# Low halves of 68 projection weights: kept in DRAM by the context's mixer, loaded again by the latents' mixer

## The chip, the core and the metric

The kernel runs on one core of a Trainium2 chip. TensorE (PE) multiplies matrices, VectorE (DVE) and ScalarE (ACT) do elementwise work, GpSimd (POOL) issues the indirect gathers and a few other transfers, and SyncE (SP) issues most loads. The metric is the device time of one execution in microseconds (us); smaller is better.

## The reference, cut to what matters

Two layers run over 512 latent tokens and 256 context tokens of width 1024. Each layer has a mixer and then a product-key expert layer ("PEER").

```
p  = h  @ w_in[l]                      # latents, 512 tokens
pc = hc @ w_in[l]                      # context, 256 tokens, the same weights (layer 0)
ml_c, state = mlstm(pc, zero_state)    # the context's scan state goes into the latents' scan
ml_x, _     = mlstm(p, state)
y = sum over 4 branches z_i of sigmoid(gate_i(p)) * (z_i @ w_branch[i]);  out = y @ w_out
x = x + mod * out
...
e, g = product-key top-16 of 128 x 128 keys, for each of 8 heads      # 128 rows per token
a = gelu(u_tab[e] . h) * g;  x = x + mod * (a @ v_tab[e])             # PEER
```

In layer 0 the context goes through the whole mixer too, with the weights that the latents use. In layer 1 the context needs only the scan state.

## The kernel before

Every weight of a mixer product is multiplied in two parts: `hi` is the fp32 weight cast to fp32r, `lo` is what the cast lost, also in fp32r. The activations are split in the same way (tiles `hh` and `hl`), and `mm3` issues three passes for each 128 rows of contraction: hi by hi, hi by lo, lo by hi.

`wload` brings one weight tile of 128 x 1024 fp32 (512 KB): a load on SP's queue into `wr`, `S.copy` (ACT) into `wh`, and `V.tensor_tensor` (DVE) into `wl`, with L299 and L300 in `split`. In both mixers of layer 0 the rings `wr`, `wh` and `wl` have three buffers each (`W_MIX`).

A tile scheduler fixes the order of the instructions on each engine when the program is built; at run time every engine works through its list in order and waits where it must. The program of layer 0 runs so:

1. The context's mixer (`mlstm`, then `ctx_merge`), with 256 columns per matmul: 68 calls of `wload`. In the middle of it `x_first` loads the latents on POOL's queue: `x`, and eight tiles `tB<-in_scT` (L233), two at a time, which DVE adds to `x`.
2. The context's `routing` (top-k). `s_bg` runs `mlstm_steps`, the first projections of the latents' mixer, beside it.
3. The latents' mixer, with 512 columns per matmul: the mLSTM scan (L452, L453) and its eight head steps, the four projections of `conv`, then four calls of `merge_one`. A call has eight gate projections, each evicted by ACT's sigmoid (`sg`), and two branch weights; `gmlp` and `fnet` come between the calls. `w_out` is last. This is again 68 calls of `wload`, on the same 68 tiles.
4. `peer_lat`, and then layer 1.

Beside 2 and 3 run the context's expert rows (`gather_ctx`), paced by `rows_bg`. Each `DMA_INDIRECT` of POOL brings 128 rows, 512 KB, into `ug` (a ring of 3) or `gat` (a ring of 9). DVE reduces each u tile against `hn` (L1034, 1.2 us), and PE accumulates the v tiles (L1068). These instructions stand at fixed places among the mixer's.

```
def tick(self, us):
    self.credit += us * self.rate
    while self.q and self.credit >= self.q[0][1]:
        self.credit -= self.q[0][1]
        self.step()
```

Of the kernel before, what the change touches and what calls it, by code (L numbers as in the profile page):

```python
# [11 lines left out]
F32 = mybir.dt.float32  # L12
# [49 lines left out]
def build(nc, tc, I, out):  # L62
    V, S, G, PE = nc.vector, nc.scalar, nc.gpsimd, nc.tensor
# [4 lines left out]
    pw = [None, 0, 0]  # L68
    pb = pool(name="pb", bufs=1)
    pd = pool(name="pd", bufs=2, space=bass.MemoryType.DRAM)  # L70
# [63 lines left out]
    class Background:  # L134
# [20 lines left out]
# [5 lines that stand above are left out]
            if not self.q:  # L160
                self.credit = 0.0
# [27 lines left out]
    def mk(p, shape, dt=F32, tag=None, bufs=None):  # L189
        nid[0] += 1  # L190
        kw = {} if bufs is None else {"bufs": bufs}
        return p.tile(list(shape), dt, name=f"{tag}_{nid[0]}", tag=tag, **kw)
# [74 lines left out]
    def held(d):  # L267

        if hold[0] is not None:
            tc.add_manual_dep(d.ins, hold[0].ins.name, SYNC, reason="leave the memory to the loads before")  # L270
# [27 lines left out]
    def split(hi, lo, src):  # L298
        S.copy(hi, src)  # L299
        V.tensor_tensor(lo, src, hi, ALU.subtract)  # L300

    def wload(src, kt, n):

        raw = mk(pw[0], [128, kt, n], F32, "wr", pw[1])
        held(nc.sync.dma_start(raw, src.rearrange("p (k n) -> p k n", n=n)))
        hi = mk(pw[0], [128, kt, n], F32R, "wh", pw[2])
        lo = mk(pw[0], [128, kt, n], F32R, "wl", pw[2])
        split(hi, lo, raw)
        tick(5.1 * T_of[0] / 512)
        return hi, lo  # L310

# [459 lines left out]
    def branch(i, l, C, h, T, tag="z"):  # L771
        ztag[0] = tag
        return BRANCH[i](l, C, h, T)

    def merge_one(l, i, first, y, z, h, T, gates=None):

        for half in range(2):
            wb = wload(I["w_branchT"][l, i, half], 2, 512)
            for q in range(4):
                dt = 4 * half + q  # L780
                if not gates:
                    sg = mk(pt, [128, T], F32, "sg")
                elif q % 2:
                    sg = sg2[:, 1]
                else:
                    sg2 = mk(gates[0], [128, 2, T], F32, gates[1 + dt // 2])
                    sg = sg2[:, 0]
                S.activation(sg, proj_T(l, h, OFF_G + i * D + 128 * dt, T), AF.Sigmoid)
                ps = psum()
                mm3(ps[:, :T], cols(wb, 128 * q, 128), z)  # L790
                if first:
                    V.tensor_tensor(y[:, dt, :], ps[:, :T], sg, ALU.mult)
                else:
                    V.tensor_tensor(sg, ps[:, :T], sg, ALU.mult)
                    V.tensor_tensor(y[:, dt, :], y[:, dt, :], sg, ALU.add)

    def y_parts(y, T):
        yh = mk(hpool[0], [128, KT, T], F32R, "hh")
        yl = mk(hpool[0], [128, KT, T], F32R, "hl")
        for k in range(KT):  # L800
            split(yh[:, k, :], yl[:, k, :], y[:, k, :])
        return [(yh[:, k, :], yl[:, k, :]) for k in range(KT)]

    def w_out(l, yp, mod, s, T, x_old, x):

        for dt in range(KT):
            w = wload(I["w_outT"][l, dt], KT, 128)
            ps = psum()
            mm3(ps[:, :T], cols(w, 0, 128), yp)
            V.scalar_tensor_tensor(x[:, dt, :], ps[:, :T], mod[:, 16 + dt, s:s + 1], x_old(dt),  # L810
                                   op0=ALU.mult, op1=ALU.add)
# [505 lines left out]
    @phase  # L1317
    def ctx_merge(l, C, mod, xc, hc, zc_fn, between, mod_ready):
        y = mk(ph[0], [128, KT, CTX], F32, "y")
        zpool[0] = ph[0]  # L1320
        end = conv(l, C, hc, CTX, ph[0])
        zs = {i: branch(i, l, C, hc, CTX, "z%d" % i) for i in (3, 1)}
        merge_one(l, 3, True, y, zs[3], hc, CTX)
        between()
        merge_one(l, 1, False, y, zs[1], hc, CTX)
        merge_one(l, 2, False, y, end(), hc, CTX)
        merge_one(l, 0, False, y, zc_fn(), hc, CTX)
        yp = y_parts(y, CTX)
        mod_ready()
        w_out(l, yp, mod, 1, CTX, lambda dt: xc[:, dt, :], xc)  # L1330
# [5 lines left out]
    with psum_pool(mm=3, sm=3, acc=2):  # L1336
# [3 lines left out]
        with spool("cxa", 1) as cxa:  # L1340
# [6 lines left out]
            use_bufs(cx, cx, CTX)  # L1347
            hc = norm_mod(xc, CTX, mod, 1, C["norm1_g"], 0)
            ada_bg.rate = ADA_RATE
            side[0] = "right"  # L1350
            zc, state = mlstm(0, C, hc, CTX, None, True, True, "zm")
            hold[0] = None
# [7 lines left out]

            hl = []
            ctx_merge(0, C, mod, xc, hc, lambda: zc, lat_norm, lambda: ada_bg.finish(ag[2]))
            cx_cm.__exit__(None, None, None)
            cx_cm, cx = open_pool("cx", "left")
            use_bufs(cx, cx, CTX)
# [216 lines left out]
```

## Time and profile before

| | us |
|---|---|
| median of 3 runs | 4453.28 (4445.75 to 4458.83) |
| the profiled execution | 4470.13 |
| its span, first to last instruction | 4468.4 |
| PE busy in it | 4184.9 (94%) |
| DVE busy in it | 3314.7 (74%) |
| DMA's mean rate over the span | 266 GB/s |

Busy time says how long an engine had work in it, not that it set the pace. A matmul of PE counts as busy until its modelled end. What a stretch is bound by is read from its own rows: the busy time of each engine in that stretch, the share of the 16 DMA engines that were busy, and the waits.

### The profile page before, as it was taken

The numbers are of one execution on the slowest core, as the hardware profiler recorded it, in microseconds if no ns is written. First come the engines' busy times: TensorE is split into PE (matmuls) and PEld (weight loads), VectorE is DVE, ScalarE is ACT, GpSimd is POOL, SyncE is SP. The second block draws the span as 40 slices with busy tenths as digits, with TensorE's granted clock in tenths as the row PEclk, the third lists the DMA queues.
The fourth block names the chain that finished last, engine by engine and source line by source line (L and its number), as shares of the span: only waits on it lengthen the run. The fifth ranks groups of instructions, "written<-read, shape, count | busy, mean of one in ns | idle before, by whom it ended". The sixth has DMA issues, their size and how long they took to land.

```text
span 4468.4 us, 61238 instructions
## 1 busy us (share of the span) xinstructions
PE 4184.9 (94%) x22364; PEld 3462.8 (77%) x22364; DVE 3314.7 (74%) x6764; ACT 1631.7 (37%) x2317; POOL 1314.7 (29%) x1061
## 2 busy tenths in 40 slices
PE   7889778988999999999999999999999999999998
PEld 4786555666678898788888766777799997888887
DVE  4764888866689596777777794464899996777775
ACT  3441222323334445333333332443335553333333
POOL 0000256652243430333333365000022222233231
PEclk9999868999999999999999999889999999999999
DMA  8546778986678996999989799213267889898894
GB/s 281 198 142 207 273 254 332 364 305 221 203 269 300 343 343 245 346 332 324 320 310 321 285 326 327 85 42 110 73 249 289 281 293 329 306 314 305 312 312 159
DMA packets 417342, 1187.41 MB, mean 266 GB/s; under 512 B 39441, under 2 KB 142609, under 8 KB 413969
## 3 DMA queue, kind: packets, MB, share of 16 engines
q1 hardware_dynamic: 263360, 633.62, 41.4%
q0 software_dynamic: 150928, 549.52, 34.1%
q8 instruction: 176, 2.88, 0.3%
q14 instruction: 126, 1.02, 0.1%
q10 hardware_dynamic: 2752, 0.37, 0.1%
HBM read 1092.40 MB, written 90.96 MB: 265 GB/s over the span
## 4 chain that ended last, share of the span: by engine, by line
PE 48%; issue 17%; DVE 12%; DMA 10%; POOL 6%; ACT 1%; POOLq 0%; DVEq 0%; another core or an unknown queue 0%; ACTq 0%; SPq 0%
PE mm L319 18%; PE s L319 12%; PE acc L1208 8%; POOL gat L924 4%; DMA gsr<-sp 3%; PE sm L1127 3%; PE acc L1068 2%; DMA vr<-in_peer_v 2%; DVE wl L300 2%; DMA gat<-in_peer_v,eu 1%; POOL ug L924 1%; PE mm L826 1%; DMA ug<-in_peer_u,hu 1%; DVE gat L955 1%; PE sm L835 1%
## 5 line engine op out<-in xcount | busy, mean ns | idle before, releaser
L299 ACT CAST wh<-wr 128x1024 fp32r<-128x1024 f32 x498 | 521.4, 1048 | 1140.5 <-PE mm L319 631.4
L300 DVE TENSOR_TENSOR wl<-wr,wh 128x1024 fp32r<-128x1024 f32 x498 | 607.2, 1220 | 322.4 <-ACT wh L299 298.3
L319 PE MATMUL s<-hh,wh 128*128 128x384 f32 x2048 | 702.1, 343 | 6.3 <-ACT gs L1151 6.3
L924 POOL DMA_INDIRECT gat<-in_peer_u,eu x256 | 329.2, 1286 | 1278.8 <-DVE pu L868 488.1
L319 PE MATMUL s<-hh,wl 128*128 128x384 f32 x2048 | 694.7, 339 | 3.6 <-DVE wl L300 3.6
L319 PE MATMUL s<-hl,wh 128*128 128x384 f32 x2048 | 693.1, 338 | 0.0
L1208 PE MATMUL acc<-vh,al 128*128 128x512 f32 x1536 | 604.6, 394 | 19.9 <-DVE al L300 19.8
L319 PE MATMUL mm<-hh,wl 128*128 128x512 f32 (+1 forms) x1552 | 582.9, 376 | 40.3 <-DVE wl L300 40.2
L319 PE MATMUL mm<-hh,wh 128*128 128x512 f32 (+1 forms) x1552 | 589.0, 381 | 24.2 <-ACT wh L299 8.3
L1208 PE MATMUL acc<-vl,ah 128*128 128x512 f32 x1536 | 603.2, 393 | 7.2 <-DVE vl L300 7.2
L1208 PE MATMUL acc<-vh,ah 128*128 128x512 f32 x1536 | 601.3, 393 | 9.1 <-ACT vh L299 7.9
L319 PE MATMUL mm<-hl,wh 128*128 128x512 f32 (+1 forms) x1552 | 582.7, 376 | 3.4 <-DVE hl L300 2.3
L924 POOL DMA_INDIRECT gat<-in_peer_v,eu x256 | 330.2, 1290 | 654.6 <-PE acc L1208 553.8
L299 ACT CAST vh<-vr 128x1024 fp32r<-128x1024 f32 x256 | 268.8, 1050 | 551.3 <-DMA vr<-in_peer_v 528.7
L924 POOL DMA_INDIRECT gat<-in_peer_v,ev x256 | 295.8, 1155 | 405.0 <-PE acc L1068 242.6
L319 PEld LDWEIGHTS s<-hh,wh 128*128 128x128 f32 x2048 | 386.3, 189 | 30.5 <-issue 10.9
L319 PEld LDWEIGHTS mm<-hh,wh 128*128 128x128 f32 x1552 | 304.6, 197 | 115.8 <-issue 20.9
L319 PEld LDWEIGHTS s<-hl,wh 128*128 128x128 f32 x2048 | 386.5, 189 | 3.5
L319 PEld LDWEIGHTS s<-hh,wl 128*128 128x128 f32 x2048 | 386.0, 188 | 4.0 <-DVE wl L300 3.9
L973 DVE SCALAR_TENSOR_TENSOR hn<-gat,a,hn 128x1024 f32<-128x1024 f32 x254 | 325.2, 1280 | 84.7 <-DMA gat<-in_peer_v,eu 84.0
L319 PEld LDWEIGHTS mm<-hh,wl 128*128 128x128 f32 x1552 | 303.7, 196 | 104.2 <-DVE wl L300 45.4
L300 DVE TENSOR_TENSOR vl<-vr,vh 128x1024 fp32r<-128x1024 f32 x256 | 312.9, 1222 | 89.9 <-ACT vh L299 88.0
(378 smaller groups left out, 6990.2 us busy)
## 6 DMA issues: line engine op xcount, KB each, us to landing
wr<-in_peer_uT SPq DMA_DIRECT2D x256, 512.0 KB
vr<-in_peer_v SPq DMA_DIRECT2D x256, 512.0 KB
wr<-in_w_inT SPq DMA_DIRECT2D x134, 512.0 KB
wada<-in_w_adaT SPq DMA_DIRECT2D x96, 512.0 KB
gd<-gt SPq DMA_DIRECT2D x24, 2048.0 KB
gr<-gd SPq DMA_DIRECT2D x64, 768.0 KB
sp<-gs SPq DMA_DIRECT2D x78, 384.0 KB
gsr<-sp SPq DMA_DIRECT2D x78, 384.0 KB
```

The lines of the kernel that those rows point to most:

```text
L299: S.copy(hi, src)
L300: V.tensor_tensor(lo, src, hi, ALU.subtract)
L319: PE.matmul(ps, w[k][a], x[k][b], start=first and k == 0 and i == 0, stop=last and k == n - 1 and i == 2)
L826: after[0] = PE.matmul(ps[:, :T], w[:, k, :], h[k][0], start=k == 0, stop=k == KT - 1)
L835: PE.matmul(ps[:, b * 128:(b + 1) * 128], qs[:, b * 128:(b + 1) * 128], C["keysT"][:, j % 2, :], start=True, stop=True)
L924: d = G.indirect_dma_start(out=t, out_offset=None, in_=tab, in_offset=bass.IndirectOffsetOnAxis(ap=ix, axis=0))
L955: V.scalar_tensor_tensor(t, t, 1.0, hn, op0=ALU.mult, op1=ALU.mult, accum_out=a[:, i:i + 1])
L973: V.scalar_tensor_tensor(on, t, a[:, i:i + 1], on, op0=ALU.mult, op1=ALU.add)
L1068: PE.matmul(po[32 * m:32 * m + 32, :], dg[:, m % 2, r, :], t[m % 2][:, 512 * (m // 2):512 * (m // 2) + 512], start=n == 0, stop=n == 31, t ...
L1127: PE.matmul(ps[:, 128 * i:128 * i + 128], o2[:, i].rearrange("p a b -> p (a b)"), o1[:, i, :], start=True, stop=True)
L1208: mm = PE.matmul(acc[b][half], a[p][:, ts], v[q][:, ds], start=done == 0 and n == 0, stop=done == 127 and n == 2)
```

## The change

While the context's mixer runs, `wload` also writes each `lo` tile to a DRAM tile of its own (`low_parts`), by a transfer on POOL's queue. When the latents' mixer asks for the same weight, `wload` loads the fp32 weight as before and casts it on ACT to `wh`. It then loads the kept `lo` tile on SP's queue, into another buffer of the same three-buffer ring `wr`, and ACT copies it to `wl`. DVE's subtraction is not issued for these 68 tiles. Layer 1 and all other loads are as before.

```diff
--- before.py
+++ after.py
@@ -299,13 +299,25 @@
         S.copy(hi, src)
         V.tensor_tensor(lo, src, hi, ALU.subtract)
 
+    keep_low, low_parts = [None], {}
+
     def wload(src, kt, n):
 
         raw = mk(pw[0], [128, kt, n], F32, "wr", pw[1])
         held(nc.sync.dma_start(raw, src.rearrange("p (k n) -> p k n", n=n)))
         hi = mk(pw[0], [128, kt, n], F32R, "wh", pw[2])
         lo = mk(pw[0], [128, kt, n], F32R, "wl", pw[2])
-        split(hi, lo, raw)
+        key = (src.tensor.name, src.offset)
+        if keep_low[0] is None and key in low_parts:
+            S.copy(hi, raw)
+            rest = mk(pw[0], [128, kt, n], F32, "wr", pw[1])
+            nc.sync.dma_start(rest, low_parts.pop(key))
+            S.copy(lo, rest)
+        else:
+            split(hi, lo, raw)
+            if keep_low[0] and key not in low_parts:
+                low_parts[key] = kept = mk(keep_low[0], [128, kt, n], F32, "lo%d" % len(low_parts), 1)
+                nc.gpsimd.dma_start(kept, lo.bitcast(F32))
         tick(5.1 * T_of[0] / 512)
         return hi, lo
 
@@ -1347,6 +1359,7 @@
             use_bufs(cx, cx, CTX)
             hc = norm_mod(xc, CTX, mod, 1, C["norm1_g"], 0)
             ada_bg.rate = ADA_RATE
+            keep_low[0] = pd
             side[0] = "right"
             zc, state = mlstm(0, C, hc, CTX, None, True, True, "zm")
             hold[0] = None
@@ -1360,6 +1373,7 @@
 
             hl = []
             ctx_merge(0, C, mod, xc, hc, lambda: zc, lat_norm, lambda: ada_bg.finish(ag[2]))
+            keep_low[0] = None
             cx_cm.__exit__(None, None, None)
             cx_cm, cx = open_pool("cx", "left")
             use_bufs(cx, cx, CTX)
```

The scheduler orders the new program anew. In the rows below a tile has the program's name and a number, and the part behind `<-` is what the instruction reads. In the new program the lines behind L300 are 12 or so higher, so L319 of `mm3` is L331, and the two casts of the loaded weight are L312 (`wh`) and L315 (`wl`).

DVE, in the latents' mixer, in front of the first scan of the mLSTM gates (the last row of each piece). `ug` and `gat` are gathered u rows, `xp` the gates' projections. Before:

```order
L1034 SCALAR_TENSOR_TENSOR ug_5376,ha_889_4614<-ug_5376,hn_4624 128x1024
L568 COPY cs_5428<-cst_764 64x65
L689 MEMSET cz_5873 128x2x15
L690 MEMSET cz_5873 128x2x15
L300 TENSOR_TENSOR wl_5928<-wr_5925,wh_5927 128x1024
L1034 SCALAR_TENSOR_TENSOR gat_5191,ha_889_4614<-gat_5191,hn_4624 128x1024
L300 TENSOR_TENSOR wl_5975<-wr_5972,wh_5974 128x1024
L465 TENSOR_SCALAR xp_5178<-mm_5244,ml_gate_b_118 64x512
L1034 SCALAR_TENSOR_TENSOR gat_5209,ha_889_4614<-gat_5209,hn_4624 128x1024
L466 TENSOR_TENSOR xp_5178<-xp_5178,tA_5269 64x512
L1034 SCALAR_TENSOR_TENSOR gat_5379,ha_889_4614<-gat_5379,hn_4624 128x1024
L452 SCALAR_TENSOR_TENSOR tB_5275<-ones_77,xp_5178 32x128
```

and now:

```order
L1046 SCALAR_TENSOR_TENSOR ug_5362,ha_963_4762<-ug_5362,hn_4772 128x1024
L702 MEMSET cz_6029 128x2x15
L1046 SCALAR_TENSOR_TENSOR ug_5368,ha_963_4762<-ug_5368,hn_4772 128x1024
L470 TENSOR_SCALAR xp_5329<-mm_5374,ml_gate_b_118 64x512
L477 TENSOR_SCALAR xp_5330<-mm_5400,ml_gate_b_118 64x512
L488 COPY m_5449<-mst_785 32x1
L489 COPY m_5449<-mst_785 32x1
L478 TENSOR_TENSOR xp_5330<-xp_5330,tA_5425 64x512
L1046 SCALAR_TENSOR_TENSOR gat_5345,ha_963_4762<-gat_5345,hn_4772 128x1024
L464 SCALAR_TENSOR_TENSOR tB_5431<-ones_77,xp_5330 32x128
```

The two subtractions into `wl` are gone, and so are the others before them; 28 reductions of u rows now stand in front of the first scan, where 32 did.

PE, at the end of the mLSTM heads: `sm<-ident,hacc` turns the heads' output, `mm<-zm` is the first branch weight of the first `merge_one`, and `mm<-hh` and `mm<-hl` are gate projections. Before:

```order
L638 MATMUL sm_5861<-ident_71,hacc_5348 128x128 x4
L638 MATMUL sm_5862<-ident_71,hacc_5348 128x128 x4
L319 MATMUL mm_6147<-zm_6065,wh_6076 128x512
L319 MATMUL mm_6156<-hh_2064,wh_6159 128x512
L319 MATMUL mm_6156<-hl_2065,wh_6159 128x512
L319 MATMUL mm_6147<-zm_6065,wh_6076 128x512
L319 MATMUL mm_6147<-zm_6065,wl_6077 128x512
L319 MATMUL mm_6147<-zm_6065,wh_6076 128x512 x2
L319 MATMUL mm_6147<-zm_6065,wl_6077 128x512
L1068 MATMUL acc_5698<-gat_6080,gat_5811 32x512
L319 MATMUL mm_6098<-hh_2064,wl_6102 128x512
L319 MATMUL mm_6098<-hh_2064,wh_6101 128x512
```

and now:

```order
L650 MATMUL sm_6017<-ident_71,hacc_5504 128x128 x4
L650 MATMUL sm_6018<-ident_71,hacc_5504 128x128 x4
L1080 MATMUL acc_5854<-gat_6191,gat_5967 32x512
L1080 MATMUL acc_5854<-gat_6152,gat_5967 32x512
L1080 MATMUL acc_5854<-gat_6191,gat_5967 32x512
L331 MATMUL mm_6315<-zm_6229,wh_6240 128x512
L331 MATMUL mm_6324<-hh_2124,wh_6327 128x512
L331 MATMUL mm_6324<-hl_2125,wh_6327 128x512
L331 MATMUL mm_6324<-hh_2124,wl_6328 128x512
L331 MATMUL mm_6324<-hh_2124,wh_6327 128x512
L331 MATMUL mm_6324<-hl_2125,wh_6327 128x512
L331 MATMUL mm_6315<-zm_6229,wh_6240 128x512
```

Before, 22 of the 24 matmuls of the first gate projection (`mm_6098`) begin here with the last two of these rows. Now they stand ahead of the transposes, among the head steps, together with the 22 of conv's fourth projection that stood among the last head steps; the rows here are of the second gate already.

ACT, in the first `merge_one` of the latents: `sg` is the sigmoid of a gate projection. Before:

```order
L299 CAST wh_6216<-wr_6214 128x1024
L788 ACT_TABLE_LOAD
L788 ACTIVATE sg_6097<-mm_6098 128x512
L299 CAST wh_6274<-wr_6272 128x1024
L788 ACTIVATE sg_6155<-mm_6156 128x512
L299 CAST wh_6329<-wr_6327 128x1024
L788 ACTIVATE sg_6212<-mm_6213 128x512
L299 CAST wh_6351<-wr_6349 128x1024
L788 ACTIVATE sg_6270<-mm_6271 128x512
L299 CAST wh_6408<-wr_6406 128x1024
```

and now:

```order
L312 CAST wh_6446<-wr_6444 128x1024
L800 ACT_TABLE_LOAD
L800 ACTIVATE sg_6323<-mm_6324 128x512
L315 CAST wl_6447<-wr_6449 128x1024
L312 CAST wh_6503<-wr_6501 128x1024
L800 ACTIVATE sg_6382<-mm_6383 128x512
L315 CAST wl_6504<-wr_6506 128x1024
L312 CAST wh_6527<-wr_6525 128x1024
L800 ACTIVATE sg_6442<-mm_6443 128x512
L315 CAST wl_6528<-wr_6530 128x1024
```

Each cast into `wl` stands behind the sigmoid that follows its own `wh`, and ahead of the next weight's `wh`.

## Rows read from the trace of the kernel before

**Rows 1.** The page: the chain that ended last, its share by engine.

```profile
PE 48%; issue 17%; DVE 12%; DMA 10%; POOL 6%; ACT 1%; POOLq 0%; DVEq 0%; another core or an unknown queue 0%; ACTq 0%; SPq 0%
```

**Rows 2.** Stretches of layer 0: busy us, PEclk, DMA share, GB/s.

```profile
core 0: us, PE busy (x) PEld busy (x) DVE busy (x) ACT busy (x) POOL busy (x), PEclk, DMA share, GB/s
464.00:507.00 43.00, 41.23 (x243) 26.29 (x243) 41.67 (x161) 13.31 (x19) 0.00 (x0) 1.00 0.81 293
507.00:593.00 86.00, 56.12 (x378) 43.63 (x375) 70.45 (x169) 28.19 (x60) 50.58 (x37) 0.78 0.78 258
593.00:728.00 135.00, 93.00 (x410) 63.50 (x409) 112.14 (x246) 28.13 (x65) 77.04 (x67) 0.63 0.77 263
728.00:780.00 52.00, 52.00 (x241) 35.61 (x240) 48.07 (x73) 11.59 (x14) 40.62 (x32) 1.00 1.00 386
728.00:860.00 132.00, 127.41 (x652) 89.83 (x651) 124.38 (x208) 41.66 (x53) 94.70 (x76) 1.00 0.99 379
860.00:960.00 100.00, 89.00 (x362) 58.17 (x362) 58.22 (x89) 22.78 (x35) 55.08 (x47) 0.93 0.83 299
960.00:1055.00 95.00, 79.52 (x347) 62.14 (x345) 80.63 (x125) 27.82 (x35) 64.07 (x48) 0.90 0.92 333
1055.00:1110.00 55.00, 53.69 (x230) 42.45 (x231) 28.89 (x38) 17.24 (x24) 0.94 (x1) 1.00 0.44 139
200.00:350.00 150.00, 133.79 (x1062) 127.92 (x1062) 87.28 (x131) 69.21 (x104) 0.91 (x1) 0.93 0.51 156
728.00:1055.00 327.00, 295.94 (x1359) 210.14 (x1357) 263.23 (x420) 92.26 (x122) 213.85 (x169) 0.95 0.92 341
```

**Rows 3.** The chain that ended last, within 860 to 1055 us, by line.

```profile
by line: issue 45.3%; POOL ug L924 22.1%; POOL gat L924 14.5%; DMA ug<-in_peer_u,hu 11.3%; DMA ond<-gat 3.0%; DVE ug L1034 1.9%; DVE wl L300 0.6%; POOL gat L1062 0.5%; DVE cz L300 0.4%; POOL hn L1024 0.3%; POOLq L924 0.3%; DVEq L300 0.0%; D
```

**Rows 4.** DVE's split L300 in two stretches: busy us, PEclk, DMA share, GB/s.

```profile
464.00:530.00 66.00, 8.54 (x7) 0.97 0.79 279
530.00:593.00 63.00, 6.04 (x5) 0.73 0.79 259
```

**Rows 5.** PE's waits, 507 to 728 us: total, times, longest.

```profile
PE mm L319 <- DVE wl L300: 26.1, 2, 22.8
```

**Rows 6.** The chain at 728 us: start, duration, what.

```profile
727.87 0.97 PE acc L1068 x2
728.85 5.33 PE mm L319 x22
```

**Rows 7.** DMA, 728 to 1055 us: totals, queue q1, weight loads issued.

```profile
DMA packets 31177, 111.56 MB, mean 341 GB/s; under 512 B 3469, under 2 KB 3469, under 8 KB 31159
q1 hardware_dynamic: 7056, 23.60, 20.0%
wr<-in_w_inT SPq DMA_DIRECT2D x31, 512.0 KB
wr<-in_w_branchT SPq DMA_DIRECT2D x7, 512.0 KB
wr<-in_w_inN SPq DMA_DIRECT2D x2, 512.0 KB
```

**Rows 8.** DVE and ACT groups, 728 to 1055 us: busy, mean ns | idle before.

```profile
L1034 DVE SCALAR_TENSOR_TENSOR ug<-ug,hn 128x1024 f32<-128x1024 f32 x85 | 103.2, 1221 | 40.6 <-DMA ug<-in_peer_u,hu 37.4 <-DMA hn<-hnd 2.8
L300 DVE TENSOR_TENSOR wl<-wr,wh 128x1024 fp32r<-128x1024 f32 x41 | 49.9, 1218 | 5.3 <-ACT wh L299 5.3
L299 ACT CAST wh<-wr 128x1024 fp32r<-128x1024 f32 x41 | 42.9, 1048 | 187.7 <-PE mm L319 146.2 <-issue 41.6
```

**Rows 9.** POOL's u gathers into `ug`, 860 to 1055 us.

```profile
L924 POOL DMA_INDIRECT ug<-in_peer_u,hu x55 | 72.1, 1311 | 44.5 <-DVE ug L1034 33.5 <-issue 10.7 <-DVE rstd L341 0.3
```

**Rows 10.** POOL's waits before 520 us: total, times, longest.

```profile
POOL tB L233 <- DVE x L234: 23.1, 4, 11.6
```

**Rows 11.** DMA, 200 to 350 us (the context's mixer): totals, queue q1.

```profile
DMA packets 6498, 23.42 MB, mean 156 GB/s; under 512 B 814, under 2 KB 814, under 8 KB 6486
q1 hardware_dynamic: 5902, 20.98, 46.2%
```

**Rows 12.** A store to DRAM of 256 KB on the chain: start, duration.

```profile
945.58 5.76 DMA ond<-gat
```

## The prediction, made before the changed kernel ran

> **What bounds the kernel now.** I read the page's chain first [rows 1]: PE holds 48% of the time that ended last, DVE 12%, DMA 10%. That is an average over stages, so I cut layer 0 into stretches [rows 2] and asked in each who is full. Five matter.
>
> - 200 to 350 us, the context's mixer: PE is busy 133.8 of 150 us, the DMA engines half (share 0.51, 156 GB/s). PE is the bound, and there is room for transfers.
> - 464 to 507 us, routing with the latents' first projections: PE 41.2 and DVE 41.7 of 43. Both are full.
> - 507 to 728 us, mLSTM scan and heads beside the first gathers: DVE is the fullest (70.5 of 86, then 112.1 of 135), PE is not.
> - 728 to 860 us, the merges begin: PE 127.4 and DVE 124.4 of 132, and the DMA share is 0.99 at 379 GB/s. Everything is full.
> - 860 to 1055 us: the chain runs almost wholly through POOL's gathers and their transfers [rows 3], with the DMA share at 0.83 and 0.92.
>
> So the change takes work from DVE in the stretches where DVE is full, and puts transfers into stretches where the DMA engines are full too. The question is which of the two is worth more. I work out differences against the profiled execution (4470.13 us, of which 4468.4 is the span) and apply the sum to the median of 4453.3, which lies 16.9 lower.
>
> **A. The stores in the context's mixer.** Added: 68 transfers of 512 KB (0.524 MB each) on POOL's queue, which is nearly empty there (0.91 us busy in 150). At 200 to 350 us the weight queue moves 20.98 MB, 40 tiles [rows 11]; as many stores bring 23.42 MB to about 44.4 MB, 296 GB/s, below the 386 that the DMA engines kept up from 728 to 780 us [rows 2]. A `wl` buffer now comes free only when its store has landed. A store of half the size took 5.76 us in a loaded stretch [rows 12]; three buffers at some 3 us of PE per weight (24 matmuls) give 9 us. PE's work is the cover; if it fails, DVE's next split is late, then PE. The store also makes POOL wait for DVE's `lo`, and behind it stand the eight `scT` loads, which already waited 23.1 us on DVE [rows 10], and later `x`, `xd` and `xcd`. Bounds: nothing, and +23 if all of that wait is passed on to the splits. I take +4, near the lower end, because PE is the bound there and DMA half idle.
>
> **B. DVE without the splits up to the first scan.** Removed: 12 subtractions, 8.54 + 6.04 = 14.6 us [rows 4]. From 464 to 507 PE is as full as DVE, so these give little. From 507 on, DVE is in front: PE once stood 22.8 us for a `wl` that waited in DVE's list behind gathered rows [rows 5], and the gate scan stood behind all of it. The order shows four u reductions fewer ahead of the scan (4 x 1.22 = 4.9 us), but they come soon after. Lower bound -14.6, upper bound 0 (if the gathers, not DVE, set the pace). I take -8, the seven splits from 507 on. What is late next is the gathers: DVE comes sooner to rows that have not landed.
>
> **C. Two projections that move.** The order puts 44 matmuls (conv's fourth projection and the first gate) ahead of the end of the heads, where PE waits for DVE. The 22 of the gate lay on the chain with 5.33 us [rows 6]. The other 22 lay among the head steps, worth another 5.33 us at most. Bounds -10.7 and 0; I take -5, the part that the chain shows.
>
> **D. The loads of the kept halves, 728 to 1055 us.** Added: one load of 0.524 MB for each of 31 + 7 + 2 = 40 weight loads issued there, 21.0 MB on top of 111.56 MB [rows 7], together 132.5 MB. Bounds: if the DMA engines were kept as busy as at 728 to 780 us, 132.5 MB / 386 GB/s = 343 us, +16 against 327. If the stretch keeps its mean of 341 GB/s [rows 2], 132.5 / 341 = 389, +62. Nothing excludes that single transfers, not the sum of them, pace part of the stretch; so for a rival I let it go down to 0.
>
> To choose, I split it at 860 us. Ahead of that the DMA share is 0.99, so the 18 added loads (9.4 MB at 379 GB/s) cost 25 us of transfer with no idle to go into. I take off 5, since gathers issued a little ahead give some slack: +20. Behind it, 22 loads (11.5 MB at 386 GB/s) cost 30 us, and the idle is 17% of 100 and 8% of 95 us, 25 us together. I let half of it be used: +18. DVE's relief is taken off there: it waited 37.4 us for landing u rows [rows 8], and POOL waited 33.5 us for DVE to free `ug` buffers [rows 9]. That loop is mostly transfer; with 1.22 us fewer in DVE's list for each of about 22 weights, a third of 27 us, some 8, may come back. 20 + 18 - 8 = +30.
>
> The Trainium skill's page "DMA: Bandwidth & Descriptors" (section "Specifications") gives an HBM limit of about 358 GB/s for a core. By that figure the stretch would need at least 370 us, an estimate of +43 from that page; the rows with 386 GB/s over 52 us stand against it as a ceiling for a core alone.
>
> **E. What costs nothing.** ACT gets 41 casts more in D's stretch, about 41 x 1.05 = 43 us [rows 8] on 92.3 of 327; it has room. Each `wl` cast makes ACT wait for the kept half; behind it stand the next `wh` cast and the sigmoids that free PE's banks. The order leaves slack: the cast follows the sigmoid of a projection two weights earlier, so about one weight, 8 us, remains before PE needs it. Without that cover each late load costs PE its lateness. In the ring `wr` two loads per weight halve the reach of the prefetch; SP's list holds nothing behind them that is due sooner than weights, except fnet's tables. From 1055 to 1110 us (`w_out`) the DMA share is 0.44, so eight more loads fit; the same order of cover holds. From there on nothing is changed.
>
> **Sum.** +4 - 8 - 5 + 30 = +21: 4470.1 to 4491 for the profiled execution, and 4453.3 + 21 = 4474 for the median.
>
> **The rivals.**
>
> *The DVE relief wins (faster).* In favour: DVE is the fullest engine from 507 to 860 us, and B and C at their bounds give -14.6 - 10.7 = -25. The gathers from 860 us on may be bound by the time of one transfer and not by the total rate, in which case the extra loads go into the 25 us of idle. With D at +5 and A at 0 this gives -20, 4433 us. It decides when D is below about 12 us. Against it: a share of 0.99 at 728 to 860 us.
>
> *It evens out (no change).* Shorter stretches up to 728 us pay for longer ones behind: B and C at -17 between them, D at its full-rate bound of +16, A near nothing. 4453 us.
>
> *The transfers cost all that they can (clearly slower).* If the gather loop keeps losing every byte's time, D is +62; with A at +18 because stores hold up the splits, and B and C at -13, that is +67, 4520 us. In favour: the loop of `ug` waits on single transfers, whose time grows when two loads share the engines with it.
>
> That the change doesn't do what it says is out: the order shows 68 stores, 68 casts into `wl` on ACT, and 68 subtractions gone.
>
> **How the numbers follow.** Forecast case (+8 to +48, 4461 to 4501): 0.45. The transfers cost all: 0.13. Evens out: 0.23. DVE relief wins: 0.19. What a measurement of this kernel can tell from no change is about 0.3%, 13 us. Nearly all of the forecast case above 4467 and all of the costliest are slower: 0.57 with a margin for the forecast case's lower edge, which lies within. The same: 0.25. Faster: 0.18. The range reaches down past the faster rival's middle and up to the costliest one's: 4432 to 4520. The forecast case's own range stands in it.
>
> **What the profile would show.** For A: PE waits in the context's mixer as before, the GB/s there nearly doubled, and no split waiting for a buffer behind a store. For B: the first scan 5 to 15 us earlier, counted from the end of routing, and the 22.8 us wait of PE gone. For C: no gate matmuls in front of the first merge. For D: the stretch from the first merge to `w_out` 340 to 375 us long, at a DMA share near 1, with more waits of PE and DVE on gathered rows; ACT's waits on the kept halves not passed on to PE. I am wrong if that stretch keeps its 327 us (the transfers fit), if the context's mixer stretches by over 10 us, or if the rows after 1110 us move.

## The result, and the profile after

The changed kernel took 4516.59 us (median of 4 runs, 4505.36 to 4520.69), the kernel before 4456.06 (4 runs). The ratio is 1.0134 with a 95% interval of 1.0111 to 1.0156: some 60 us slower. The forecast was 4474, with a range that ends at 4520. The sign was right and the size was a third of what came.

I cut the profile at four events that both programs have: POOL's store of `xcd` (the context is done), the cast of `zm` (the first merge begins), the first write of `xl` (`w_out` begins to end), and the end. The starts of these instructions give:

| stretch, us | before | after | difference | forecast |
|---|---|---|---|---|
| start to the `xcd` store | 352.9 | 386.8 | +33.9 | A: +4 |
| `xcd` store to `zm` | 371.1 | 361.6 | -9.5 | B and C: -13 |
| `zm` to the first `xl` | 366.9 | 394.9 | +28.0 | D: +30 |
| up to the first `xl` | 1090.9 | 1143.3 | +52.4 | +21 |

Behind the first `xl` only four of the kept halves are still loaded, and the rest of the code is that of before. There the one profiled execution of before took 3377.5 us of its span, and that of after 3367.7; the other profiles of this study start their first output store 3350 to 3363 us after the first `xl`, that of before 3369.7. So the profiled execution of before took 7 to 20 us longer behind the first `xl` than the others do. Against the profile of after it is 10 us, of the 18 us by which the difference of the two spans, 42.6 us, lies below that of the medians.

So one term of four is wrong, and it is the one that I priced lowest. In the context's mixer DVE's waits now read as follows (waits of DVE, 40 to 387 us of the changed kernel: total, times, longest).

```profile
DVE wl L300 <- DMA lo<-wl: 56.1, 21, 6.4
DVE wl L300 <- ACT wh L299: 21.6, 15, 4.7
```

The first row is new: 21 splits of 68 waited 56.1 us for a store to land. Before, the split waited only for ACT's `wh` (DVE's waits, 40 to 353 us):

```profile
DVE wl L300 <- ACT wh L299: 55.3, 38, 4.0
```

So DVE's waits in front of `wl` grew from 55.3 to 77.7 us, by 22 and not by 56: in part it now waits for a store where it waited for ACT. A piece of DVE's timeline of the changed kernel shows such waits (in brackets the idle time ahead and what ended it).

```profile
319.16 1.23 DVE L300 TENSOR_TENSOR wl<-wr,wh 128x1024 fp32r<-128x1024 f32 x1 [2.56 <-DMA lo<-wl]
...
323.13 1.23 DVE L300 TENSOR_TENSOR wl<-wr,wh 128x1024 fp32r<-128x1024 f32 x1 [1.95 <-DMA lo<-wl]
...
324.61 1.22 DVE L300 TENSOR_TENSOR wl<-wr,wh 128x1024 fp32r<-128x1024 f32 x1
...
330.04 1.22 DVE L300 TENSOR_TENSOR wl<-wr,wh 128x1024 fp32r<-128x1024 f32 x1 [3.88 <-DMA lo<-wl]
...
332.63 1.23 DVE L300 TENSOR_TENSOR wl<-wr,wh 128x1024 fp32r<-128x1024 f32 x1 [0.57 <-DMA lo<-wl]
```

The ring has three buffers, but here only two of them take turns. `merge_one` loads one branch weight and then four gate weights, and the branch weight's `wl` is read beside all four. The split at 319.16 filled it, and PE reads it until 338.82 (PE's timeline):

```profile
322.39 0.28 PE L331 MATMUL mm<-zm,wl 128*128 128x256 f32 x1
...
338.82 0.28 PE L331 MATMUL mm<-zm,wl 128*128 128x256 f32 x1
```

So the split at 330.04 needs the buffer that the split at 323.13 filled, and that of 332.63 the one of 324.61. The semaphores in the trace say the same: in 20 of the 21 waits, what ends the wait is the store of the second split before, not of the third. The chain that ended last has one. Of the splits at 340.86, 342.33 and 349.22, the third starts when the store behind the first, issued at 342.38, has landed at 349.03:

```profile
342.38 6.65 DMA lo<-wl
...
349.22 1.23 DVE wl L300
```

In those 20 waits the split starts 6.7 to 9.4 us after the one that filled its buffer, 8.0 in the median. Windows of the changed kernel, columns as in [rows 2]: the context's mixer, and the merges in three pieces.

```profile
200.00:350.00 150.00, 119.41 (x929) 112.19 (x927) 77.06 (x115) 62.09 (x90) 21.85 (x40) 0.91 0.80 268
749.00:881.00 132.00, 124.91 (x612) 81.86 (x610) 98.11 (x174) 51.98 (x65) 81.38 (x73) 1.00 1.01 393
881.00:981.00 100.00, 90.22 (x358) 55.89 (x351) 44.60 (x73) 29.39 (x41) 43.65 (x43) 0.93 0.95 360
981.00:1107.00 126.00, 94.00 (x390) 73.17 (x389) 83.04 (x139) 46.39 (x57) 72.17 (x60) 0.84 0.94 353
```

From 200 to 350 us PE is busy 119.4 us, where it was 133.8, and the DMA engines move 268 GB/s, not 156; the share is 0.80, so they are not full on the mean. From 40 us to the `xcd` store PE's 2082 matmuls keep it busy 289.5 of 347 us at a mean granted clock of 0.90 of full speed; before, it was 279.9 of 313 us at 0.93. So of the 34 us, some 24 are idle time of PE and 10 are the same matmuls taking longer. Behind the first merge the rate went up everywhere: 393 GB/s over 132 us (379 before), and the gaps of 860 to 1055 us [rows 2] are mostly filled, with shares of 0.95 and 0.94.

What that does to the merges shows in the groups of the stretch from `zm` to `xl` (busy, mean ns | idle before and its releasers).

```profile
L1046 DVE SCALAR_TENSOR_TENSOR ug<-ug,hn 128x1024 f32<-128x1024 f32 x86 | 104.9, 1224 | 89.5 <-DMA ug<-in_peer_u,hu 85.8 <-DMA hn<-hnd 3.5
L936 POOL DMA_INDIRECT ug<-in_peer_u,hu x85 | 100.2, 1179 | 109.5 <-DVE ug L1046 93.0 <-issue 8.6 <-DMA gat<-in_peer_v,ev 5.4
...
L312 ACT CAST wh<-wr 128x1024 fp32r<-128x1024 f32 x45 | 47.3, 1051 | 160.0 <-PE mm L331 106.2 <-issue 44.5 <-DMA wr<-in_w_inT 4.9
L315 ACT CAST wl<-wr 128x1024 fp32r<-128x1024 f32 x45 | 46.9, 1042 | 34.5 <-DMA wr<-lo 34.5
```

DVE waits 85.8 us for u rows to land, where it waited 37.4 [rows 8]; POOL waits 93.0 us for DVE to free `ug`, where it waited 37.6 from 724 to 1091 us, 33.5 of them behind 860 [rows 9]. The subtractions are gone, and DVE does nothing else with the time: it stands longer in front of the same gathers. The chain of waits from 860 to 1107 us says the same.

```profile
by line: DMA ug<-in_peer_u,hu 29.4%; issue 28.0%; POOL ug L936 13.2%; DMA gat<-in_peer_v,ev 12.8%; POOL gat L936 4.5%; PE mm L331 3.8%; DVE ug L1046 2.5%; DMA ond<-gat 2.4%; ACT wh L312 0.8%; ACT L800 0.5%; DVE gat L1046 0.5%; PE acc L1080 
```

The landing of u rows holds 29.4% of it (25.8% from 884 on, which lies as far behind the first merge as 860 did before), against 11.3% before [rows 3].

### The profile page after: what moved, and what is told of

The parts are those of the page before. It is cut to its first block, busy times and chain, and to the rows that moved or that the text cites. A ratio compares the mean times of both kernels' runs of the same rounds, so it can differ in the third digit from the quotient of the medians.

```text
span 4511.0 us, 61555 instructions
## 1 busy us (share of the span) xinstructions
PE 4197.9 (93%) x22364; PEld 3457.8 (77%) x22364; DVE 3244.5 (72%) x6696; ACT 1698.1 (38%) x2385; POOL 1339.8 (30%) x1129
## 4 chain that ended last, share of the span: by engine, by line
PE 44%; issue 21%; DMA 16%; DVE 12%; POOL 5%; ACT 1%; POOLq 0%; DVEq 0%; SPq 0%; ACTq 0%
PE mm L331 14%; PE s L331 13%; PE acc L1220 8%; PE sm L1139 4%; DMA ug<-in_peer_u,hu 3%; DMA gsr<-sp 3%; POOL gat L936 3%; DMA vr<-in_peer_v 2%; DVE wl L300 2%; PE acc L1080 2%; DMA gat<-in_peer_v,eu 2%; DMA gat<-in_peer_u,hu 1%; DMA gat<-in_peer_v,ev 1%; DVE gat L967 1%; POOL ug L936 1%
## 5 line engine op out<-in xcount | busy, mean ns | idle before, releaser
L299 ACT CAST wh<-wr 128x1024 fp32r<-128x1024 f32 x430 | 450.3, 1048 | 890.8 <-PE mm L331 414.5
L300 DVE TENSOR_TENSOR wl<-wr,wh 128x1024 fp32r<-128x1024 f32 x430 | 524.4, 1220 | 325.8 <-ACT wh L299 265.7
L331 PE MATMUL s<-hh,wh 128*128 128x384 f32 x2048 | 702.4, 343 | 7.5 <-ACT gs L1163 7.5
L331 PE MATMUL s<-hh,wl 128*128 128x384 f32 x2048 | 694.8, 339 | 3.4 <-DVE wl L300 3.4
L331 PE MATMUL s<-hl,wh 128*128 128x384 f32 x2048 | 693.0, 338 | 0.0
L331 PE MATMUL mm<-hh,wh 128*128 128x512 f32 (+1 forms) x1552 | 587.2, 380 | 36.6 <-DVE sg L806 13.9
L331 PE MATMUL mm<-hh,wl 128*128 128x512 f32 (+1 forms) x1552 | 580.2, 375 | 16.9 <-DVE wl L300 14.6
L331 PE MATMUL mm<-hl,wh 128*128 128x512 f32 (+1 forms) x1552 | 581.7, 375 | 3.4 <-DVE hl L300 2.7
L936 POOL DMA_INDIRECT gat<-in_peer_v,eu x256 | 344.5, 1346 | 643.6 <-PE acc L1220 540.1
L331 PEld LDWEIGHTS s<-hh,wh 128*128 128x128 f32 x2048 | 386.2, 189 | 32.8 <-issue 10.9
L331 PEld LDWEIGHTS mm<-hh,wh 128*128 128x128 f32 x1552 | 302.7, 195 | 132.0 <-issue 25.3
L331 PEld LDWEIGHTS s<-hl,wh 128*128 128x128 f32 x2048 | 386.3, 189 | 3.5
L331 PEld LDWEIGHTS s<-hh,wl 128*128 128x128 f32 x2048 | 385.8, 188 | 3.8 <-DVE wl L300 3.8
L300 DVE TENSOR_TENSOR vl<-vr,vh 128x1024 fp32r<-128x1024 f32 x256 | 312.6, 1222 | 82.0 <-ACT vh L299 81.3
L331 PEld LDWEIGHTS mm<-hh,wl 128*128 128x128 f32 x1552 | 302.8, 195 | 81.0 <-DVE wl L300 17.9
```

The costliest lines, as they stand in the source:

```text
L331: PE.matmul(ps, w[k][a], x[k][b], start=first and k == 0 and i == 0, stop=last and k == n - 1 and i == 2)
L936: d = G.indirect_dma_start(out=t, out_offset=None, in_=tab, in_offset=bass.IndirectOffsetOnAxis(ap=ix, axis=0))
```

## The experiments

**Theories.** For the context: *(a)* a split waits for its `wl` buffer, held by a store; *(b)* the stores' bytes, or their places in POOL's list, slow loads that the context needs. For the merges: *(c)* the bytes of the kept halves delay the gathers; *(d)* the cost is not the bytes but the buffers that they take from `wr`, or ACT's in-order list with two casts in front of each sigmoid. For the relief: *(e)* it pays only where DVE and not the gathers set the pace, ahead of the first merge; *(f)* it pays behind it too.

The stretches are those of the table above, from each kernel's own profile. Each ratio is to runs of before on the same chip (their medians 4456 to 4463 us). The first column varies by 7 us between kernels that do the same there (348.7 to 355.6).

| kernel | to `xcd` | `xcd` to `zm` | `zm` to `xl` | median us | ratio to before (95%) |
|---|---|---|---|---|---|
| before | 352.9 | 371.1 | 366.9 | 4456.06 | |
| the change | 386.8 | 361.6 | 394.9 | 4516.59 | 1.0134 (1.0111 to 1.0156) |
| 1 stores alone | 387.9 | 367.2 | 373.2 | 4488.17 | 1.0072 (1.0048 to 1.0095) |
| 2 loads and relief | 348.7 | 367.5 | 398.2 | 4476.08 | 1.0038 (1.002 to 1.0055) |
| 3 relief alone | 353.3 | 354.8 | 367.3 | 4437.24 | 0.9947 (0.9928 to 0.9967) |
| 4 loads, and split | 354.7 | 380.4 | 409.8 | 4506.79 | 1.011 (1.0085 to 1.0136) |
| 5 six buffers | 359.6 | 365.9 | 393.7 | 4489.81 | 1.0075 (1.0057 to 1.0094) |
| 6 relief, 4 KB loads | 353.5 | 354.0 | 374.0 | 4452.42 | 0.9995 (0.9985 to 1.0004) |
| 7 relief, 256 KB loads | 353.0 | 357.5 | 386.9 | 4478.17 | 1.0053 (1.0032 to 1.0073) |
| 8 relief, 512 KB loads | 350.8 | 367.6 | 402.4 | 4486.19 | 1.0069 (1.0052 to 1.0086) |
| 9 first 14 weights | 356.6 | 370.4 | 362.5 | 4460.59 | 0.9991 (0.9973 to 1.0008) |
| 10 first 10 weights | 354.4 | 364.4 | 369.8 | 4452.22 | 0.9979 (0.9964 to 0.9995) |
| 11 loads into `wl` | 364.2 | 367.9 | 395.3 | 4493.47 | 1.0088 (1.0072 to 1.0104) |
| 12 no second cast | 355.6 | 352.4 | 365.0 | 4444.87 | 0.9972 (0.9957 to 0.9986) |

**1, stores alone.** The latents' mixer computes its own low halves.

```diff
-        if keep_low[0] is None and key in low_parts:
+        if False:
```

> Stores alone: the context's mixer keeps its 68 low halves in DRAM, the latents' mixer computes its own as before. Theory (the stores hold the wl buffers): the context ends as late as in the changed kernel, its xcd store at about 387 us against 353, and nothing is given back, so about +34 us, 4490. First scan and first merge then also some 34 later than before (628 and 759), and the stretch from the first merge to the first xl write keeps its 366 us. Rival (the 34 us come from the new order of the whole program, not from the stores): the context ends near 353 and the time is within 13 us of before.

The `xcd` store comes at 387.9, 35 us late, and the median moves by +31. The lateness of the context reaches the end of the kernel. That the new order of the latents' mixer did it is out.

**2, loads without stores.** Only the first tile is stored; the latents' mixer is that of the change, with its loads and its relief of DVE.

```diff
-                low_parts[key] = kept = mk(keep_low[0], [128, kt, n], F32, "lo%d" % len(low_parts), 1)
-                nc.gpsimd.dma_start(kept, lo.bitcast(F32))
+                if not low_parts:
+                    kept = mk(keep_low[0], [128, kt, n], F32, "lo", 1)
+                    nc.gpsimd.dma_start(kept, lo.bitcast(F32))
+                else:
+                    kept = next(iter(low_parts.values()))
+                low_parts[key] = kept
```

> Loads alone: only the first low half is stored, and all 68 loads of the latents' mixer read that one tile (this leaves out the true low parts of the other 67 weights; bytes, buffers and instructions of the latents' mixer are those of the change). Theory (the two costs are separate): the context ends at 353 as before, first scan and first merge come about 9 us earlier than before (585 and 716), and first merge to first xl write takes about 394 us against 366; the sum is +19, about 4475. Rival (the loads cost little and only the lateness from the context reaches the end): first merge to xl stays within 8 us of 366, and the time is at or below before.

As the theory had it: +18 in the median, and 398 us from `zm` to `xl`. The medians of 1 and 2 add to 49 of the 60 us, and in the profiles their delays at the first `xl` (+37.4 and +23.5) to 61 against 52; within what single executions vary by, the two costs are separate. The first scan came 13.5 us earlier; 4.2 of them lie ahead of the `xcd` store, within that column's spread, and 9.3 behind it, as expected. The heads behind the scan took 5.7 us longer.

**3, relief alone.** As 2, and:

```diff
-            rest = mk(pw[0], [128, kt, n], F32, "wr", pw[1])
-            nc.sync.dma_start(rest, low_parts.pop(key))
-            S.copy(lo, rest)
+            low_parts.pop(key)
+            S.copy(lo, raw)
```

> DVE's relief alone: no stores but one, no extra loads; ACT copies the raw weight to wl (this leaves out the true low part of the latents' 68 weights; the work of PE is the same). Theory (the relief is worth its share ahead of the first scan and a few us behind): scan and first merge about 9 us earlier than before, first merge to xl about 358 against 366, the sum -17, about 4440. Rival (the relief is worth nothing where the gathers set the pace): only the 9 us, about 4447. A second rival (DVE is the bound of all of 507 to 860 us): -30 or more, below 4426.

The relief is worth 20 us in the median, and in the profile 16 of them lie ahead of the first merge. Behind it the stretch is 367.3 us, as before, though DVE has 52 us less to do there (234.9 us busy in 367, in the windows below, against 287.0 in 366). So theory (e) holds, and the 8 us that the forecast gave the relief in the merges were not there.

**4, loads without relief.** As 2, but DVE splits as before and the loaded tile is dropped.

```diff
-            S.copy(hi, raw)
+            split(hi, lo, raw)
             rest = mk(pw[0], [128, kt, n], F32, "wr", pw[1])
             nc.sync.dma_start(rest, low_parts.pop(key))
-            S.copy(lo, rest)
```

> The extra loads alone: the latents' mixer loads a kept low half into wr for each of its 68 weights (all from one stored tile), drops it, and still splits on DVE; so nothing is left out of the result. Theory (bytes and ring buffers are the cost behind the first merge): first merge to xl write 394 us or a little more, since the relief is missing, and nothing gained before the first scan: +28 to +36, 4481 to 4490. Rival (the cost is the wait of ACT for the kept half, with the sigmoids behind it, and not the bytes): first merge to xl within 8 us of 366, the time within 13 us of before.

This came out dearer than the theory said: +49 in the median, +43 from `zm` to `xl`. It differs from kernel 2 by 11.6 us there, so beside the loads the relief does pay something. DVE's waits of kernel 4, from 735 to 1145 us, show where:

```profile
DVE ug L1049 <- DMA ug<-in_peer_u,hu: 49.6, 28, 5.5
DVE wl L300 <- ACT wh L299: 44.8, 15, 6.8
```

A weight that lands late holds `wh`, and DVE stands 44.8 us in front of `wl`, with the u rows' reductions queued behind it; without the loads that wait was 17.6 us from 724 to 1090, 5.3 of them ahead of `w_out` [rows 8]. In the change the same lateness falls on ACT (34.5 us for `wl`, in the groups above), where no reduction is queued. ACT does not wait for the kept half here, and the time is longer, so that wait is not what the loads cost; kernel 8 shows the same without the splits.

**5, a ring of six for `wl` in the context.** The whole change, with

```diff
-        lo = mk(pw[0], [128, kt, n], F32R, "wl", pw[2])
+        lo = mk(kl[0] or pw[0], [128, kt, n], F32R, "wl", 6 if kl[0] else pw[2])
@@ around the context's mixer
+            kl_cm, kl[0] = right_pool("kl")
+            keep_low[0] = kl[0] = None
+            close_right(kl_cm)
```

> The change with one thing more: while the context's mixer runs, wl comes from a ring of six buffers of its own; nothing is left out. Theory (a split waits for its wl buffer behind the store that still reads it, 56 us in 21 waits in the changed kernel): these waits go to under 10 us, the xcd store comes at 353 to 363 us, not 387, and the time is 25 to 34 us below the changed kernel, 4483 to 4492. Rival (the stores' bytes slow the weight loads, or POOL's list in order makes x and scT late): the xcd store stays beyond 375 and the time above 4500.

DVE's waits in front of `wl` in the context's mixer, as a group (40 to 387 us of this kernel):

```profile
L300 DVE TENSOR_TENSOR wl<-wr,wh 128x1024 fp32r<-128x1024 f32 x68 | 83.0, 1223 | 56.7 <-ACT wh L299 56.1 <-DMA lo<-wl 0.4
```

56.1 us of waits for stores became 0.4 (the other 56.1 are waits for ACT's `wh`, the 55.3 of before). The same 68 stores of the same bytes go on the same queue, and the context ends 27 us earlier, at 359.6; the median is 27 us below the change. Theory (a) explains 27 of the 34 us. Six buffers without stores were not run; they should give little, since no split of before waited for a buffer. The rest, 7 us here and 11 in kernel 11, whose context is the same, is left for the bytes and for the spread of this column.

**6, 7 and 8, how the price goes with the bytes.** Kernel 3 with one more load into `wr` for each weight, that nobody reads: 32 bytes, half, or all of each partition's row.

```diff
-            low_parts.pop(key)
+            rest, kept = mk(pw[0], [128, kt, n], F32, "wr", pw[1]), low_parts.pop(key)
+            nc.sync.dma_start(rest[:, :1, :8], kept[:, :1, :8])
             S.copy(lo, raw)
```

In 7 the slices are `[:, :kt // 2, :]` and `[:, :kept.shape[1] // 2, :]`, in 8 the whole tiles.

> The kernel with DVE's relief alone, and beside each of the latents' 68 weight loads one more load into the ring wr of 4 KB (32 bytes for each partition) that nobody reads; the true low parts are left out. Theory (bytes are the cost): first merge to first xl write 367 to 373 us, as without it, time about 4440. Rival (the buffer that the load takes from the ring of three, and so the prefetch, is the cost): 385 us or more, the time near 4460 to 4475.

> As with the 4 KB load, but 256 KB for each weight, unread; the true low parts are left out. Theory (bytes): half way, first merge to first xl write about 380 to 385 us, the time about 4455 to 4458. Rival (a threshold: the first half fits into the idle of the DMA engines): 367 to 372 us and 4440. Rival (ring): no different from the 4 KB load.

> As with the 4 KB load, but the whole 512 KB for each weight, unread: ACT casts from the raw tile and never waits for the kept half; the true low parts are left out. Theory (bytes): first merge to first xl write 394 to 400 us, as in the kernel with the loads alone, the time about 4474. Rival (ACT's wait for the kept half, with sigmoids behind it, is the cost): 367 to 375 us, and 4440 to 4448.

From `zm` to `xl` the four kernels 3, 6, 7 and 8 take 367.3, 374.0, 386.9 and 402.4 us. The buffer of `wr` and the load as such cost 6.7 us, the first half of the bytes 12.9, the second 15.5. Half of the bytes already cost, so no threshold hides them, and bytes hold 28 of the 35 us. Kernel 8, where ACT never waits for the kept half, takes no less than kernel 2. The bytes cost ahead of the first merge too: `xcd` to `zm` goes from 354.0 to 357.5 and 367.6.

The medians (4437, 4452, 4478, 4486) came 12 to 22 us above what I expected of 6, 7 and 8. Their steps are 15, 26 and 8 us, where the profiles at the first `xl` have 6, 16 and 23: the profiled executions of 6 and 7 lie among the shortest of their runs, those of 3 and 8 among the longest. By both, bytes are most of the price (34 of 49 and 39 of 45 us). How much the buffer of `wr` costs by itself is not settled closer than 6 to 15 us.

The windows of the same stretches of kernels 3, 6, 7 and 8 (columns as in [rows 2]):

```profile
708.00:1075.00 367.00, 331.95 (x1501) 232.22 (x1500) 234.94 (x404) 144.34 (x185) 210.25 (x174) 0.95 0.88 318
```

```profile
707.00:1081.00 374.00, 335.41 (x1501) 233.94 (x1501) 235.39 (x404) 144.59 (x185) 203.73 (x175) 0.94 0.87 311
```

```profile
710.00:1097.00 387.00, 338.30 (x1502) 235.89 (x1501) 235.54 (x404) 144.55 (x185) 199.97 (x174) 0.93 0.90 331
```

```profile
718.00:1121.00 403.00, 343.27 (x1504) 238.16 (x1503) 235.59 (x405) 145.18 (x186) 201.52 (x176) 0.92 0.91 347
```

Rate and time rise together from 6 to 8, 311 to 347 GB/s (the last column) and 374 to 403 us. The gathers land later as the bytes grow: from issue to landing a transfer into `ug` takes 6.5, 6.7, 7.4 and 7.9 us in the median of kernels 3, 6, 7 and 8, and DVE waits 40.2, 44.0, 46.9 and 55.0 us for them. Of the 35 us between kernels 3 and 8, 11 are the same matmuls keeping PE busy for longer, at a mean granted clock of 0.92 instead of 0.95; the rest is idle time of PE. Half of the added transfer goes into gaps, half into time: the change moves 140.0 MB between `zm` and `xl` and before 117.6; the 22.4 MB would take 58 us at 386 GB/s, and the stretch grew by 28.

**9 and 10, only the weights that come back ahead of the first merge.** Kernel 5, keeping the first 14 (in 10: the first 10).

```diff
-            if keep_low[0] and key not in low_parts:
+            if keep_low[0] and key not in low_parts and len(low_parts) < 14:
```

> The change for the first 14 weights alone (the mLSTM's ten and conv's four, used again before the first merge), with the six-buffer ring for wl in the context's mixer; the other 54 are split by DVE as before, and nothing is left out. Theory (relief pays only ahead of the first scan, bytes cost only behind the first merge, stores cost only where they hold a buffer): xcd store at 350 to 358 us, first scan 8 to 14 us earlier counted from it, first merge to first xl write 366 to 374, time -5 to -12, about 4447. Rival (14 stores in the context's first stretch, where ada's weights fill the DMA engines, and 14 loads beside the first gathers cost what the relief gives): within 5 us of before, or slower.

> The same for the first ten weights alone, the mLSTM's; conv's four are split as before, and nothing is left out. Theory: most of the gain ahead of the first scan is kept (10 of 13 splits), first scan 6 to 12 us earlier counted from the xcd store, and no added load stands beside the heads: time -5 to -10, 4446 to 4451. Rival: as for the 14.

The 14 give no measurable gain: 0.9991, with 1 inside the interval. The 10 are 0.21% faster than before, with an interval that ends at 0.9995. In kernel 10 the first scan came 14.7 us earlier counted from the `xcd` store, but the heads behind it took 138.3 us, not 130.3. The windows from the scan to the first merge, of before, kernel 10 and kernel 12, say why:

```profile
593.00:724.00 131.00, 89.00 (x399) 60.66 (x398) 108.94 (x242) 26.96 (x63) 73.65 (x65) 0.63 0.77 260
```

```profile
580.00:719.00 139.00, 88.71 (x404) 62.35 (x403) 118.78 (x260) 29.54 (x66) 80.75 (x68) 0.63 0.77 266
```

```profile
581.00:708.00 127.00, 84.81 (x410) 57.25 (x409) 110.12 (x246) 31.25 (x66) 75.55 (x64) 0.69 0.81 279
```

DVE has 118.8 us of work there in kernel 10, where before had 108.9: three splits and five reductions of gathered rows more, some 10 us. Work that stood ahead of the scan was put behind it, and DVE is busy for 83 to 87% of this stretch in all three, so about half of the gain was only moved. Kernel 12, which has no splits here, keeps it.

**11, the kept half loaded straight into `wl`.** Kernel 5 without the second `wr` buffer and ACT's cast.

```diff
-            rest = mk(pw[0], [128, kt, n], F32, "wr", pw[1])
-            nc.sync.dma_start(rest, low_parts.pop(key))
-            S.copy(lo, rest)
+            nc.sync.dma_start(lo.bitcast(F32), low_parts.pop(key))
```

> The change with the six-buffer ring, and with the kept half loaded straight into wl: no second buffer of wr, no cast of it on ACT; nothing is left out. Theory (bytes are nearly all of the cost behind the first merge): first merge to first xl write 385 to 398 us, time 4475 to 4490, little below the kernel with the ring alone (4490). Rival (the wr buffers and ACT's casts, with the sigmoids behind them, are half of it or more): 366 to 380 us, time below 4470.

395.3 us from `zm` to `xl`, 4493 in the median: no better than kernel 5. Taking away the second buffer of `wr` and ACT's cast gave nothing back, which agrees with the bytes as most of the price. (A load into `wl` must itself wait until PE has done with that buffer; what this costs is not measured.)

**12, relief without ACT's second cast.** As 3, with no `wl` for the latents' weights at all.

```diff
-            S.copy(lo, raw)
+            lo = hi
```

> DVE's relief without ACT's second cast: the latents' 68 weights get no low half at all, and PE multiplies by wh where wl stood (this leaves out the true low parts; PE's work is the same, one tile is kept in DRAM for form). Theory (behind the first merge the gathers and their transfers set the pace, so relief of DVE is worth nothing): first merge to first xl write 362 to 369 us, time as with the relief by ACT's copy, about 4437 to 4445. Rival (ACT's casts ahead of the sigmoids, 27 us of DVE's waits for sg, ate the relief there): 358 us or less, time below 4430.

DVE's waits of kernel 3 (708 to 1075 us) and of kernel 12 (700 to 1080 us):

```profile
DVE ug L1049 <- DMA ug<-in_peer_u,hu: 40.2, 31, 4.8
DVE sg L809 <- ACT sg L803: 27.0, 5, 9.2
DVE sg L809 <- PE mm L334: 23.5, 8, 4.2
```

```profile
DVE sg L809 <- PE mm L334: 44.3, 10, 8.6
DVE ug L1049 <- DMA ug<-in_peer_u,hu: 39.6, 23, 4.6
...
DVE sg L809 <- ACT sg L803: 4.8, 2, 3.1
```

DVE's waits for ACT's sigmoids fall from 27.0 to 4.8 us, and the stretch stays at 365.0 us. They were no cost: the wait for PE behind them grows from 23.5 to 44.3. The wait for landing u rows is 40 us in both. Theory (e) again, and the second cast on ACT is free here, as the forecast had it.

## Why the prediction was half right

**A was wrong, and it is the miss.** I put the stores at +4, with +23 as the upper bound; they cost +34 in the profile, and 31 in the median of kernel 1. The step that failed is the cover: "three buffers at some 3 us of PE per weight (24 matmuls) give 9 us", set against a store time of 5.76 us. In the merges one of the three buffers is held by the branch weight, so a gate weight has two, and two weights at 3 us of PE give 6 us. The buffer's turn is not the store alone either: it holds the split (1.2 us), POOL's issue 0.3 us behind it, and the landing, in all 6.7 to 9.4 us from split to split in 20 of the 21 waits. So the turn is longer than the cover of two buffers, and mostly shorter than the 9 us that I had counted on. The landing alone was close to my figure in the median, at twice the bytes (page, DMA issues of the changed kernel: KB each, median us to landing):

```profile
lo<-wl POOLq DMA_DIRECT2D x68, 512.0 KB, 5.9
```

I had written down what would follow if the cover fails, "DVE's next split is late, then PE", but then took the upper bound from the `scT` waits on POOL, a wait with no part in it. The bound had to come from the ring: a turn of some 8 us against 6 us of cover stops DVE, 2.7 us on the mean and 6.4 at most in the 21 waits. By the forecast's own sign, a context that stretches by over 10 us, this part was wrong. A DMA share of 0.5 said nothing against it, since what was short was buffers and not rate; kernel 5 shows that with the same stores.

**B and C together were nearly right, as a sum of a gain and a cost that I left out.** The relief ahead of the first merge is worth 16 to 19 us (kernels 3 and 12), more than the 13 I gave it. The loads there take some 13 back (354.8 in kernel 3, 367.5 in kernel 2), which I did not price: the sum had D's loads only from 728 us on, though 19 of the 68 are issued ahead of the first merge. The net was -9.5, and not all of it is the relief's: in kernel 1, without any relief, the same stretch is 3.9 us shorter than before. That the sum came near -13 is in part luck. The 22.8 us wait of PE is gone; PE's longest wait between the first gathers and the first merge is now 8.0 us:

```profile
PE sm L560 <- DVE nt L556: 20.2, 5, 8.0
```

C's order came as forecast, with no wall of gate matmuls at the first merge, but the heads took 132.2 us and not fewer than 130.3: nothing of its 5 us is to be seen in the change, at most 2 to 4 where no loads stand beside it (128.2 and 126.2 in kernels 3 and 12).

**D was right in size, and its mechanism was shown.** +28.0 against +30: the loads delay the gathers, the bytes hold 28 of 35 us between kernels 3 and 8, and half of them go into gaps. The 8 us taken off for DVE's relief were wrong as argued: without the loads the relief gives nothing there. Beside them it gives 11.6 us (kernels 4 and 2), by another way than the one I named, since a split that waits for a late weight holds up the reductions behind it. The Trainium skill's page "DMA: Bandwidth & Descriptors" (section "Specifications") has about 358 GB/s as the limit, and by it I estimated +43; the changed kernel moved 393 GB/s over 132 us, so the row decides against that limit for a core alone.

**E was right.** ACT waited 34.5 us for kept halves; kernel 8 shows that this wait costs no time, and kernel 12 that the second cast costs none.

The rival in which the transfers cost all that they can named the right place for the surplus, stores that hold up the splits, at +18 and with a chance of 0.13, and gave 4520 against 4517 measured. But its other part, +62 for D, did not happen; it was right in sum for the wrong reason.

What stays open: the 7 us by which the context is still late with six buffers, and the exact price of the `wr` buffer.

## What to carry to other kernels

A transfer that reads a tile holds the tile's buffer until it lands. Before looking at the DMA rate, count the whole turn (producer, issue, landing) against the work per tile times the buffers that really take turns, without those that a longer-lived tile of the same ring holds; if it does not fit, give such a tile a deeper ring. Engine work swapped for bytes pays only where that engine, and not transfers, sets the pace; here that was the stretch of some 240 us from the context's end to the first scan, and only part of the gain stayed. Price every load that the change adds, also in the stretches where it helps.

## What the runs showed that I had not expected

Between 749 and 881 us the changed kernel's DMA engines held a level of about 410 GB/s in most slices, above the 386 that I had taken as the full rate; the kernel before had reached 400 GB/s or more in 23 of 40 slices from 728 to 860 us too (DMA view of the changed kernel, GB/s in 40 slices of that window).

```profile
GB/s 307 322 343 309 254 364 411 413 411 407 412 410 407 413 408 403 412 408 407 411 407 411 411 403 417 400 408 413 408 401 380 358 403 418 410 407 407 404 399 406
```

And DVE's work fell by 52 us in a stretch of 367 where DVE had been busy for 78% of the time, with no change in the stretch at all (kernel 3), while the same work taken away beside 22 MB of added loads was worth 11.6 us (kernels 4 and 2).
